# A gated MLP on one core: a reordered start, w1 sums by block, 16-bit turns and a cast moved out of the first stage

## The chip, the cores and the metric

One core of one Trainium2 chip. The metric is the time of one execution in microseconds (us), as the device reports it. An execution counts as slow when it is over 1.5% above the fastest of the same kernel. Before the change the median is 311.07 us (310.92 to 311.54, three executions).

## The reference

```python
batch, seq, dim, hidden = 16, 256, 512, 2048      # x 4096 x 512, w1 512 x 4096, w2 2048 x 512, all fp32
h = x @ w1
gate, value = np.split(h, 2, axis=-1)
h = np.maximum(gate, 0) * value
return (h @ w2).astype(np.float32)
```

## The kernel before: the parts that matter here

The kernel uses a seven-product scheme (P1 to P7) in place of eight block products for both matrix products, in fp16, over four stages of 1024 rows each. It needs sums of blocks of x (S1 to S4, on VectorE or GpSimd), of w1 (T1 to T4, on GpSimd), of w2 (also T1 to T4) and of the intermediate g. Stage 0 is special: x comes straight from its fp32 rows and is turned (transposed in blocks of 128x128) on TensorE; its first two column blocks ("plain") use ordinary products, while the sums are still missing. For stages 1 to 3, GpSimd starts a casting transfer of x to fp16 in DRAM, and transposing loads bring it in.

```python
# the order of the loads before ("fetch(i)" loads the i-th piece of w1, "fetch_first(h)" four blocks of x)
fetch(0, nc.scalar)          # w1 block 0, from ScalarE's queue
fetch_first(0)               # x blocks 0 to 3, SyncE's queue
fetch(1, nc.sync)
make_identity(nc, ident)
fetch_first(1)               # x blocks 4 to 7
fetch(2, nc.sync)            # w1 blocks 2 and 3
fetch(3, nc.sync)

def turn_first(o, h, b, ps):                       # one x block: four fp32 transposes into one PSUM bank
    for e in range(4):
        nc.tensor.transpose(ps[:, e * P:(e + 1) * P], xn[h][b][:, e * P:(e + 1) * P], ident)
    for k, copy in ((0, nc.vector.tensor_copy), (1, nc.scalar.copy)):
        copy(out=o[f"A{h + 1}{k + 1}"][:, :, b * P:(b + 1) * P], in_=ps[...])

# w1 sums of two blocks at once, on GpSimd
nc.gpsimd.tensor_tensor(op["T1"], b12, b11, op=SUB)
nc.gpsimd.tensor_tensor(op["T2"], b22, (op["T1"]), op=SUB)
nc.gpsimd.tensor_tensor(op["T3"], b22, b12, op=SUB)
nc.gpsimd.tensor_tensor(op["T4"], b21, (op["T2"]), op=SUB)
# ... cut ...
CASTS = {(0, 11): 1, (0, 13): 0, (0, 14): 2, (1, 8): 3}      # (stage, block): x of which stage is cast
FIRST_ORDER = ("P1 0, P1 1, P2 0, P2 1, P1 2, P5 0, P2 2, P6 0, ...")   # second product of stage 0
```

A matmul pair of 512 columns takes 0.43 us, eight of 256 columns 0.87 us. The second product's P5 of pair 0 needs S1 of g, which VectorE computes. And in these traces every instruction of an engine waits for those before it on the same engine, so a check or a copy that is not urgent can hold one that is (at 149 us below, ScalarE's copy starts when its check of 1.05 us is over).

## Time and profile before

| What | Value | View |
|---|---|---|
| median time | 311.07 us | executions |
| PE busy | 301.5 of 309.2 us | the page, part 1 |
| PE in the chain that ended last | 93% | the page, part 4 |
| P4 of block 2 begins | 23.30 us | timeline |
| end of the last matmul | 304.56 us | chain in order of time |

These are the page's head, its busy times and the chain by engine. PE is TensorE, PEld its weight loads, DVE is VectorE, ACT ScalarE, POOL GpSimd, SP SyncE; "issue" is time in which an engine waited for nothing that the profile shows, and a q marks an engine's sequencer.

```profile
span 309.2 us, 5211 instructions
PE 301.5 (98%) x1870; PEld 183.2 (59%) x1870; DVE 236.4 (76%) x378; ACT 177.0 (57%) x350; POOL 153.7 (50%) x186
PE 93%; DVE 2%; DMA 2%; issue 1%; SPq 0%; ACT 0%; DVEq 0%
```

TensorE bounds the kernel. What is left lies in the start. The chain in order of time (start, length, what) shows the last thing that is not TensorE:

```profile
21.96 0.69 DVE g L261
22.65 0.61 DVE cc L266
23.30 0.59 PE Y L233 x2
```

From 23.30 us on this chain is TensorE alone. I call this matmul "P4 of block 2" and use it as the milestone: the end of the kernel is P4's start, plus a fixed amount of matmul work, plus the stalls after it.

Now the timeline: start, length, engine, line, operation, output from inputs, count, and in brackets the engine's idle time before it and what ended it.

```profile
6.24 0.66 PE L448 MATMUL X<-ident,x_A 128*128 128x128 f32 x4 [0.78 <-DMA x_A<-in_x_dram]
15.57 1.36 POOL L215 TENSOR_TENSOR w_T<-w_stage 128x512 f16<-128x512 f32 x1 [5.44 <-DMA w_stage<-in_w_dram]
17.39 0.59 PE L233 MATMUL X<-x_A,w_B 128*128 128x512 f16 x2
18.64 0.59 PE L233 MATMUL X<-x_A,w_B 128*128 128x512 f16 x2 [0.23 <-ACT Y L240]
23.30 0.59 PE L233 MATMUL Y<-x_A,w_T 128*128 128x512 f16 x2 [0.47 <-DVE cc L266]
...
60.18 4.06 POOL L581 TENSOR_TENSOR v_T<-v_B,v_T 128x2048 f16<-128x2048 f16 x1
64.02 0.78 DVE L164 TENSOR_TENSOR w_stage<-g 128x1024 f16<-128x1024 f16 x1
65.22 1.04 PE L333 MATMUL W<-v_T,w_stage 128*128 128x256 f16 x8
...
149.02 1.05 ACT L179 ACTIVATE sq<-w_T 128x1024 f16<-128x1024 f16 x1
150.06 0.37 ACT L360 ACTIVATE pu<-Y 128x256 f32<-128x256 f32 x1
150.48 1.03 PE L333 MATMUL Y<-v_T,w_stage 128*128 128x256 f16 x8
```

The second x block arrives at 6.2 us, and the first block with sums starts at 17.39. At 64 us VectorE's S1 of the second product (L164) begins when GpSimd's long w2 sum is nearly over, and takes 0.78 us. At 149 us ScalarE does a 1.05 us check of a weight tile (`sq`) in front of the copy (L360) that TensorE needs; the next matmul begins 0.2 us late. The same happens in the next stage at 223 us.

### The profile page before, as it was taken

What the parts mean: (1) busy time and instruction counts of PE and PEld (TensorE: products, weight loads), DVE (VectorE), ACT (ScalarE), POOL (GpSimd) and SP (SyncE); (2) the same over time, 40 slices, a digit from 0 to 9 for tenths busy, and PEclk for the clock granted to TensorE, in tenths of its full rate; (3) what the DMA queues carried; (4) which work ended last, traced back from release to release, by engine and by line L of the source; (5) the groups of instructions that cost most, each with busy time, mean ns of one, the idle gap of its engine ahead of it and who ended that gap; (6) DMA issues with size and microseconds to landing.
All of it is one profiled execution on the core that took longest, in us unless ns stands there. A gap on an engine that the chain in (4) does not pass through costs nothing.

```text
span 309.2 us, 5211 instructions
## 1 busy us (share of the span) xinstructions
PE 301.5 (98%) x1870; PEld 183.2 (59%) x1870; DVE 236.4 (76%) x378; ACT 177.0 (57%) x350; POOL 153.7 (50%) x186
## 2 busy tenths in 40 slices
PE   7999999999999999999999999999999999999994
PEld 3844444588854444478864444458884444448883
DVE  1598888889678888887538888888536888888841
ACT  2588886445865555537855555546956555553231
POOL 2199999930048899500028889700006988700000
PEclk9999999999999999999999999999999999999999
DMA  7977696998594233001354400000325110000132
GB/s 236 355 230 251 176 232 87 196 214 149 164 303 101 69 70 68 2 0 47 127 184 105 119 0 4 0 0 15 122 103 171 37 34 1 0 3 0 70 136 72
DMA packets 37340, 32.87 MB, mean 106 GB/s; under 512 B 14400, under 2 KB 32320, under 8 KB 37184
## 3 DMA queue, kind: packets, MB, share of 16 engines
q1 hardware_dynamic: 31904, 25.70, 27.2%
q0 software_dynamic: 4352, 6.29, 11.8%
q10 hardware_dynamic: 1056, 0.52, 0.6%
q8 instruction: 15, 0.25, 0.3%
q14 instruction: 13, 0.11, 0.1%
HBM read 27.26 MB, written 12.58 MB: 129 GB/s over the span
## 4 chain that ended last, share of the span: by engine, by line
PE 93%; DVE 2%; DMA 2%; issue 1%; SPq 0%; ACT 0%; DVEq 0%
PE Y L233 26%; PE X L233 17%; PE W L233 17%; PE Y L333 14%; PE X L333 9%; PE W L333 9%; DMA x_A<-in_x_dram 2%; DVE x_S L164 1%; PE X L448 1%; DVE g L308 1%; PE X L301 1%; PE W L301 1%; PE W L448 0%; PE Y L150 0%; DVE x_S L450 0%
## 5 line engine op out<-in xcount | busy, mean ns | idle before, releaser
L233 PEld LDWEIGHTS <-w_T 128*128 128x128 f16 x496 | 48.5, 98 | 57.5 <-issue 1.0
L170 POOL TENSOR_TENSOR fold<-xh 128x1024 f32<-128x1024 f16 x16 | 30.3, 1894 | 93.1 <-DMA xh<-x 92.1
L233 PE MATMUL X<-x_A,w_B 128*128 128x512 f16 x248 | 73.7, 379 | 0.2 <-ACT Y L240 0.2
L233 PE MATMUL Y<-x_S,w_T 128*128 128x512 f16 x248 | 73.8, 379 | 0.0
L233 PEld LDWEIGHTS <-w_B 128*128 128x128 f16 x372 | 36.4, 98 | 42.6 <-issue 0.8
L240 ACT COPY Y<-X 128x512 f32<-128x512 f32 x62 | 35.4, 570 | 39.8 <-PE X L233 39.5
L260 DVE SCALAR_TENSOR_TENSOR cc<-W,pu 128x512 f32<-128x512 f32 x62 | 42.8, 691 | 19.5 <-ACT pu L254 19.5
L254 ACT ACTIVATE pu<-Y 128x512 f32<-128x512 f32 x62 | 37.0, 597 | 34.1 <-PE Y L233 32.8
L173 POOL TENSOR_TENSOR fold<-fold 128x512 f32<-128x512 f32 (+2 forms) x96 | 51.8, 540 | 7.5
L333 PEld LDWEIGHTS <-w_stage 128*128 128x128 f16 x512 | 50.0, 98 | 6.3 <-issue 0.4
L266 DVE SCALAR_TENSOR_TENSOR cc<-Y,pu 128x512 f32<-128x512 f32 x62 | 42.8, 691 | 7.2 <-PE Y L233 0.7
L261 DVE SCALAR_TENSOR_TENSOR g<-X,cc 128x512 f16<-128x512 f32 x62 | 42.9, 691 | 2.3
L276 DVE SCALAR_TENSOR_TENSOR g<-Y,cc 128x512 f16<-128x512 f32 x62 | 42.2, 681 | 1.8 <-PE Y L233 1.8
L333 PEld LDWEIGHTS <-g 128*128 128x128 f16 x384 | 37.6, 98 | 8.2
L233 PE MATMUL Y<-x_A,w_T 128*128 128x512 f16 x124 | 36.9, 379 | 0.5 <-DVE cc L266 0.5
L247 ACT ACTIVATE pu<-W 128x512 f32<-128x512 f32 x62 | 37.2, 600 | 0.2 <-ACT Y L240 0.2
L233 PE MATMUL W<-x_S,w_T 128*128 128x512 f16 x124 | 36.9, 379 | 0.0
L233 PE MATMUL W<-x_S,w_B 128*128 128x512 f16 x124 | 36.9, 379 | 0.0
L333 PE MATMUL Y<-v_T,w_stage 128*128 128x256 f16 x256 | 33.2, 272 | 0.1
L333 PE MATMUL X<-v_B,g 128*128 128x256 f16 x256 | 31.9, 273 | 0.0
L164 DVE TENSOR_TENSOR w_stage<-g 128x1024 f16<-128x1024 f16 x32 | 21.5, 686 | 0.2
L365 DVE SCALAR_TENSOR_TENSOR o<-W,pu 128x256 f32<-128x256 f32 x16 | 6.7, 422 | 18.7 <-PE W L333 18.7
(84 smaller groups left out, 283.8 us busy)
## 6 DMA issues: line engine op xcount, KB each, us to landing
out_dram<-o SPq DMA_DIRECT2D x30, 256.0 KB, 2.0
w_stage<-in_w_dram SPq DMA_DIRECT2D x14, 512.0 KB, 5.7
x<-in_x_dram POOLq DMA_DIRECT2D x4, 1024.0 KB, 12.9
xh<-x SPq DMA_DIRECT2D x16, 256.0 KB, 3.1
v_B<-in_w_dram POOLq DMA_DIRECT2D x3, 512.0 KB, 6.3
x_S<-in_x_dram SPq DMA_DIRECT2D x4, 256.0 KB, 5.5
x_A<-in_x_dram SPq DMA_DIRECT2D x3, 256.0 KB, 4.9
w_stage<-in_w_dram ACTq DMA_DIRECT2D x2, 256.0 KB, 4.6
```

The costliest lines, as they stand in the source:

```text
L164: yield eng.tensor_tensor(o[n], o[i0], o[i1], op=op)
L170: nc.gpsimd.tensor_tensor(fold, t, t, op=MULT)
L173: nc.gpsimd.tensor_tensor(fold[:, :, :m], fold[:, :, :m], fold[:, :, m:2 * m], op=ADD)
L233: nc.tensor.matmul(ps, wop[wn][:, b, self.jb * P:(self.jb + 1) * P], self.xo[xn][:, b, :], start=fresh and b == 0, stop=b == 1, skip_group ...
L240: nc.scalar.copy(out=self.Y, in_=self.X)
L247: nc.scalar.activation(self.p5, self.W, COPY, scale=GS)
L254: nc.scalar.activation(self.u2, self.Y, COPY, scale=GS)
L260: nc.vector.scalar_tensor_tensor(out=self.c12, in0=self.W, scalar=GS, in1=self.u2, op0=MULT, op1=ADD)
L261: nc.vector.scalar_tensor_tensor(out=self.g[:, self.jb, :TH], in0=self.X, scalar=0.0, in1=self.c12, op0=MAX, op1=MULT)
L266: nc.vector.scalar_tensor_tensor(out=self.c22, in0=self.Y, scalar=GS, in1=self.p5, op0=MULT, op1=ADD)
L276: nc.vector.scalar_tensor_tensor(out=self.g[:, self.jb, TH:], in0=self.Y, scalar=0.0, in1=self.c22, op0=MAX, op1=MULT)
L333: nc.tensor.matmul(ps, self.op[an][:, i], vop[wn][:, i], start=name in ("P1", "P5") and i == 0, stop=i == NJ // 2 - 1, skip_group_check=True)
```

## The change

The intent is to use TensorE's holes in the first 23 us. In words: load w1 block 0 behind two x blocks, on the same queue; put parts of the plain products between turns; cast the second half of x to fp16 before turning it; take the w1 sums of blocks 2 and 3, the first that need them, one block at a time; fill waits with warm matmuls; and cast x of stage 0 (needed only for the check of its range) in stage 2. Smaller edits go along: a check moves from pair 1 to pair 2, two w2 jobs move, and more output transfers of the last stage are split. The core, cut, with comments added for the reader:

```diff
-    fetch(0, nc.scalar)
-    fetch_first(0)
+    fetch_first(0, (0, 1))
+    ws[0] = load_w1(nc.sync, *wl[0])
+    fetch_first(0, (2, 3))
     fetch(1, nc.sync)
...
+    turn_first(xo, 0, 0, [t[:, :2 * P] for t in YS], (dve, act))     # two banks for one turn
+    turn_first(xo, 0, 1, left, (dve, act))
+    rest()
+    arm(YS[0])                                                        # warm matmuls
+    arm(YS[1])
+    plain[0].open()
+    keep_busy(2)
+    plain[0].part("gate", *first_half, half)
+    keep_busy(6)
+    turn_first(xo, 0, 2, right, (dve, act))
...
+    for b in range(3):
+        cast_first(b, pool)                                           # later x as fp16
...
-    prepare(2)
-    copy_some(3)
+    prepare(2, False)                                                 # sums of w1 block 2, then 3
+    sum_w1(6)
...
+    prepare(3, False)
+    w_sums[:4] = [w_sums[i] for i in (2, 0, 3, 1)]
+    sum_w1()
...
-            if self.t < (2 if self.s else 3):
+            if self.t in ((0, 2) if self.s else (0, 1, 2)):           # where a check stands
...
-    CASTS = {(0, 11): 1, (0, 13): 0, (0, 14): 2, (1, 8): 3}
+    CASTS = {(0, 11): 1, (0, 14): 2, (1, 8): 3, (2, 3): 0}
...
-            for n2, i0, i1, at in (("T3", "B22", "T3", (46, 50)), ("T4", "B21", "T2", (57, 58))):
+            for n2, i0, i1, at in (("T3", "B22", "T3", (46, 50)), ("T4", "B21", "T2", (57, 64))):
```

More of the change, by code (lines that the diff above doesn't have):

```diff
@@ L142, in fast_way @@
     ident = wpool.tile([P, P], F32, name="ident")
+    Y = psy.tile([P, TH], F32, name="Y", tag="Y")
     for i in range(NWARM):
-        Y = psy.tile([P, TH], F32, name="Y", tag="Y")
         nc.tensor.matmul(Y, warm_b[:, :P], warm_b[:, :TH], start=True, stop=True)
@@ L159, in x_tiles, with sum_of @@
         return o
+    SUMS_X = {"S1": ("A21", "A22", ADD), "S2": ("S1", "A11", SUB), "S4": ("A12", "S2", SUB), "S3": ("A11", "A21", SUB)}
+    def sum_of(o, n, eng=nc.vector):
+        i0, i1, op = SUMS_X[n]
+        eng.tensor_tensor(o[n], o[i0], o[i1], op=op)
     def sums_of(o, eng=nc.vector):
-        for n, i0, i1, op in (("S1", "A21", "A22", ADD), ("S2", "S1", "A11", SUB), ("S4", "A12", "S2", SUB),
-                              ("S3", "A11", "A21", SUB)):
-            yield eng.tensor_tensor(o[n], o[i0], o[i1], op=op)
+        for n in SUMS_X:
+            yield sum_of(o, n, eng)
     def look(t, at):
@@ L201, in load_rows, with load_w1, w1_ops, operands @@
         return t
-    def load_w1(eng, jb, n, u):
+    def load_w1(eng, jb, n, u, vs=(0, 1)):
         t = w_stage[:, u:u + n].rearrange("p u v -> p (u v)").rearrange("p (g e j) -> p g e j", g=2, e=4)
-        for v in range(2):
+        for v in vs:
             eng.dma_start(out=t[:, v], in_=w1_v[v, :, :, jb * P:(jb + n) * P])
         return t.rearrange("p g (k b) j -> p k b g j", k=2)
-    def w1_ops(jb, n, t):
-        js = slice(jb * P, (jb + n) * P)
-        b11, b21, b12, b22 = t[:, 0, :, 0], t[:, 1, :, 0], t[:, 0, :, 1], t[:, 1, :, 1]
-        op = {n: w[:, :, js] for n, w in wop.items()}
-        nc.gpsimd.tensor_tensor(op["T1"], b12, b11, op=SUB)
-        nc.gpsimd.tensor_tensor(op["T2"], b22, (op["T1"]), op=SUB)
-        nc.gpsimd.tensor_tensor(op["T3"], b22, b12, op=SUB)
-        nc.gpsimd.tensor_tensor(op["T4"], b21, (op["T2"]), op=SUB)
+    def w1_ops(jb, n, t, m):
+        def operands(j0, m):
+            js = slice((jb + j0) * P, (jb + j0 + m) * P)
+            b11, b21, b12, b22 = (t[:, k, :, v, j0 * P:(j0 + m) * P] for v in range(2) for k in range(2))
+            return {n: w[:, :, js] for n, w in wop.items()}, b11, b21, b12, b22
+        steps = [(0, i, n) for i in range(4)]
+        if m < n:
+            steps = [(j0, i, m) for j0, i in ((0, 0), (0, 1), (m, 0), (0, 2), (m, 1), (0, 3), (m, 2), (m, 3))]
+        def step(j0, i, m):
+            op, b11, b21, b12, b22 = operands(j0, m)
+            nc.gpsimd.tensor_tensor(op[f"T{i + 1}"], (b12, b22, b22, b21)[i], (b11, op["T1"], b12, op["T2"])[i], op=SUB)
+        w_sums.extend(lambda a=a: step(*a) for a in steps)
+        op, b11, b21, b12, b22 = operands(0, n)
         return [lambda o=o, i=i: nc.scalar.copy(out=o, in_=i)
@@ L290, in __init__, with open, part @@
             self.g, self.jb = g, jb
-        def products(self, h, a1, a2, cols=(0, TH)):
+        def open(self, X=None, W=None):
+            self.X = psx.tile([P, TH], F32, name="X", tag="X") if X is None else X
+            self.W = psw.tile([P, TH], F32, name="W", tag="W") if W is None else W
+        def part(self, which, a1, a2, cols=(0, TH)):
             js, c = slice(self.jb * P, (self.jb + 1) * P), slice(*cols)
-            if cols[0] == 0:
-                self.X = psx.tile([P, TH], F32, name="X", tag="X")
-                self.W = psw.tile([P, TH], F32, name="W", tag="W")
-            for a, gate, value in ((a1, "B11", "T3"), (a2, "B21", "B22")):
-                for ps, wn in ((self.X, gate), (self.W, value)):
-                    for b in range(2):
-                        nc.tensor.matmul(ps[:, c], wop[wn][:, b, js], a[:, b, c], start=a is a1 and b == 0,
-                                         stop=a is a2 and b == 1)
+            ps, names = (self.X, ("B11", "B21")) if which == "gate" else (self.W, ("T3", "B22"))
+            for a, wn in zip((a1, a2), names):
+                for b in range(2):
+                    nc.tensor.matmul(ps[:, c], wop[wn][:, b, js], a[:, b, c], start=a is a1 and b == 0,
+                                     stop=a is a2 and b == 1)
         def value(self):
@@ L316, in __init__ @@
             self.s, self.t = s, t
-            self.end = s == NS - 1 and t == NB // 2 - 1
+            self.end = s == NS - 1 and t != NB // 2 - 2
             o = {f"A{h + 1}{u + 1}": g[:, u * NJ // 2:(u + 1) * NJ // 2, h * TH + t * P:h * TH + (t + 1) * P]
@@ L412, in fetch, with sum_w1, prepare @@
             ws[i] = load_w1(eng, jb, n, u)
-    def prepare(i):
+    w_sums = []
+    def sum_w1(n=None):
+        for job in w_sums[:n]:
+            job()
+        del w_sums[:n]
+    def prepare(i, at_once=True):
         jb, n, _ = wl[i]
-        copies.extend((i, c) for c in w1_ops(jb, n, ws.pop(i)))
+        copies.extend((i, c) for c in w1_ops(jb, n, ws.pop(i), 1 if i == 2 else n))
+        if at_once:
+            sum_w1()
     def copy_some(n):
@@ L440, in fast_way, with fetch_first, cast_first, turn_first @@
     xn = [[t.rearrange("p a b -> p (a b)").bitcast(F32) for t in place[4 * h:4 * h + 4]] for h in range(2)]
-    def fetch_first(h):
-        for b in range(4):
-            nc.sync.dma_start(out=xn[h][b], in_=x_nat[0, h, b])
-    def turn_first(o, h, b, ps):
-        for e in range(4):
-            nc.tensor.transpose(ps[:, e * P:(e + 1) * P], xn[h][b][:, e * P:(e + 1) * P], ident)
-        for k, copy in ((0, nc.vector.tensor_copy), (1, nc.scalar.copy)):
-            copy(out=o[f"A{h + 1}{k + 1}"][:, :, b * P:(b + 1) * P],
-                 in_=ps[:, k * 256:k * 256 + 256].rearrange("p (b t) -> p b t", b=2))
+    x16_first = [halfs.tile([P, 8, P], F16, name="xh", tag="xh").rearrange("p (b q) c -> p b (q c)", b=2) for _ in range(2)]
+    ident16 = wpool.tile([P, P], F16, name="ident16")
+    half, other = (0, TH // 2), (TH // 2, TH)
+    def fetch_first(h, bs):
+        for b in bs:
+            nc.sync.dma_start(out=xn[h][b], in_=x_nat[0, h, b])
+    def cast_first(b, copy):
+        copy(out=x16_first[b // 2][:, b % 2], in_=xn[1][b])
+    def turn_first(o, h, b, places, copies):
+        rows, one = (x16_first[b // 2][:, b % 2], ident16) if h else (xn[0][b], ident)
+        for k in range(2):
+            for e in range(2):
+                nc.tensor.transpose(places[k][:, e * P:(e + 1) * P],
+                                    rows[:, (2 * k + e) * P:(2 * k + e + 1) * P], one)
+        for k in range(2):
+            copies[k](out=o[f"A{h + 1}{k + 1}"][:, :, b * P:(b + 1) * P],
+                      in_=places[k].rearrange("p (b t) -> p b t", b=2))
     def new_x():
         return psx.tile([P, TH], F32, name="X", tag="X")
-    def new_w():
-        return psw.tile([P, TH], F32, name="W", tag="W")
-    fetch(0, nc.scalar)
-    fetch_first(0)
+    def new_y():
+        return psy.tile([P, TH], F32, name="Y", tag="Y")
+    def arm(ps):
+        nc.tensor.matmul(ps, warm_b[:, :P], warm_b[:, :TH], start=True, stop=True)
+    dve, act, pool = nc.vector.tensor_copy, nc.scalar.copy, nc.gpsimd.tensor_copy
+    fetch_first(0, (0, 1))
+    ws[0] = load_w1(nc.sync, *wl[0])
+    fetch_first(0, (2, 3))
     fetch(1, nc.sync)
     make_identity(nc, ident)
-    fetch_first(1)
+    fetch_first(1, range(4))
     fetch(2, nc.sync)
     fetch(3, nc.sync)
+    dve(out=ident16, in_=ident)
     xo = x_tiles()
@@ L468, in fast_way @@
     first_half, second_half = (xo["A11"], xo["A12"]), (xo["A21"], xo["A22"])
-    half, other = (0, TH // 2), (TH // 2, TH)
+    YS, XS = [new_y(), new_y()], [new_x(), new_x()]
+    left, right = ([t[:, c:c + 2 * P] for t in XS] for c in (0, 2 * P))
+    turns = [[t.bitcast(F16)[:, c:c + 2 * P] for c in (0, 2 * P)] for t in YS]
     rest = plain_w(0)
-    turn_first(xo, 0, 0, new_w())
-    keep_busy(2)
-    turn_first(xo, 0, 1, new_x())
-    rest()
-    keep_busy(4)
-    turn_first(xo, 0, 2, new_x())
@@ L477, in fast_way @@
-    keep_busy(2)
-    turn_first(xo, 0, 3, new_w())
-    keep_busy(2)
-    plain[0].products(0, *first_half, half)
-    plain_w(1)()
+    turn_first(xo, 0, 0, [t[:, :2 * P] for t in YS], (dve, act))
[4 more added lines that the diff above has]
+    plain[0].open()
+    keep_busy(2)
+    plain[0].part("gate", *first_half, half)
+    keep_busy(6)
+    turn_first(xo, 0, 2, right, (dve, act))
+    turn_first(xo, 0, 3, left, (dve, act))
+    plain[0].part("value", *first_half, half)
@@ L482, in fast_way @@
+    rest = plain_w(1)
+    plain[0].part("gate", *first_half, other)
+    plain[0].part("value", *first_half, other)
+    rest()
     fetch(4, nc.sync)
-    plain[0].products(0, *first_half, other)
     plain[0].value()
+    plain[1].open()
+    plain[1].part("gate", *first_half)
     plain[0].gate(0)
-    plain[1].products(0, *first_half, half)
-    ps = [new_x(), new_w()]
-    for b in range(4):
-        turn_first(xo, 1, b, ps[b % 2])
-        if b == 1:
-            plain[1].products(0, *first_half, other)
-            plain[1].value()
@@ L493, in fast_way @@
-    plain[1].gate(0)
-    sums = sums_of(xo)
-    prepare(2)
-    copy_some(3)
-    fetch(5, nc.sync)
-    next(sums)
-    plain[0].products(1, *second_half, half)
-    next(sums)
-    next(sums)
-    plain[0].products(1, *second_half, other)
-    plain[0].value()
-    plain[0].gate(1)
-    prepare(3)
-    plain[1].products(1, *second_half)
+    for b in range(3):
+        cast_first(b, pool)
+    plain[1].part("value", *first_half, half)
+    turn_first(xo, 1, 0, turns[1], (act, act))
+    turn_first(xo, 1, 1, turns[0], (dve, dve))
@@ new lines, in fast_way @@
+    plain[1].part("value", *first_half, other)
+    cast_first(3, dve)
+    xo["S3"] = halfs.tile([P, 8, P], F16, name="xh", tag="xh").rearrange("p (a b) c -> p a (b c)", a=2)
+    sums = [sums_of({n: t[:, :, slice(*c)] for n, t in xo.items()}) for c in (half, other)]
+    next(sums[0])
+    turn_first(xo, 1, 2, turns[1], (act, act))
+    spare = plain[0].X.bitcast(F16)[:, :2 * P]
+    plain[0].open()
+    plain[0].part("gate", *second_half, half)
+    turn_first(xo, 1, 3, (turns[0][0], spare), (dve, act))
@@ new lines, in fast_way @@
+    plain[1].value()
+    plain[0].part("value", *second_half, half)
+    next(sums[0])
+    next(sums[1])
+    next(sums[1])
+    plain[0].part("gate", *second_half, other)
+    plain[0].part("value", *second_half, other)
+    for n in ("S4", "S3"):
+        sum_of(xo, n)
+    plain[1].gate(0)
+    prepare(2, False)
+    sum_w1(6)
+    copy_some(1)
+    plain[0].value()
+    copy_some(2)
+    plain[1].open(*reversed(YS))
+    plain[1].part("gate", *second_half)
+    prepare(3, False)
+    w_sums[:4] = [w_sums[i] for i in (2, 0, 3, 1)]
@@ L508, in fast_way, with last_plain @@
+    sum_w1()
+    fetch(5, nc.sync)
+    def last_plain():
+        plain[1].part("value", *second_half)
+        plain[1].value()
+        plain[0].gate(1)
+        plain[1].gate(1)
     LOOKX, looks = {}, []
@@ L544, in fast_way @@
     for n, at in enumerate(ats):
-        LOOKX[at] = n // 4, n % 4
+        LOOKX[at] = (n // 4 + 1) % NS, n % 4
     rows = []
@@ L551, in fast_way @@
     TAIL = 4
-    CASTS = {(0, 11): 1, (0, 13): 0, (0, 14): 2, (1, 8): 3}
+    CASTS = {(0, 11): 1, (0, 14): 2, (1, 8): 3, (2, 3): 0}
     SUMS = (10, 11, 12, 13)
-    SUMS_FIRST = (10, 11, 13, 45), (17, 22, 26, 53), (33, 37, 41, 64), (67, 72, 76, 80)
+    SUMS_FIRST = (10, 11, 13, 45), (17, 22, 26, 53), (33, 37, 41, 66), (67, 72, 76, 80)
     SUMS_AT = (10, 11, 13, 15), (22, 26, 30, 36), (46, 53, 57, 61), (70, 78, 82, 87)
@@ L595, in fast_way @@
                 if s == 0 and (n, jb) == ("P1", NPLAIN):
-                    plain[1].value()
-                if s == 0 and (n, jb) == ("P5", NPLAIN):
-                    next(sums)
-                    plain[1].gate(1)
-                if n in ("P6", "P7"):
+                    last_plain()
+                if n == "P7" or (n, jb) == ("P5", NPLAIN + 1) or n == "P6" and (s, jb) != (0, NPLAIN):
                     copy_some(1)
```

## The prediction

> **What bounds the kernel.** TensorE, nearly everywhere. The page has PE busy 301.5 of 309.2 us and 93% of the chain that ended last; the chain, in order of time, is unbroken matmul work from 23.30 us (the fourth product P4 of block 2) to 304.56 us, with pieces of 0.43 us for two 512-column matmuls and 0.87 us for eight 256-column ones. The change leaves that arithmetic alone, so only the first 23.3 us and the tail can move, and the tail (last copy at 304.58, then one output transfer) is the same for the last pair.
>
> **The start before (timeline).** PE waits for x until 4.59, then for block 1 until 6.20; x turns and plain products wait on copies; block 2's P1 begins 17.39, its P2 waits 0.23 for ScalarE's copy, its P4 waits until 23.30 for VectorE's L266. PE had about 16 us of needed work between 4.6 and 23.3, with 1.1 us of warm matmuls: about 1.6 us of holes. VectorE is continuous from 13.76 to 23.25 and is what releases P4. Its x sums took 0.70 us alone (S1) but 1.65 and 1.53 us (S2, S4) once GpSimd's w1 sums had begun at 15.57. The Trainium skill ("GPSIMD Engine Reference", "Specifications") says the two engines share SBUF interfaces and contend for VectorE instructions with two SBUF inputs; this trace agrees.
>
> **What the change does.**
> - w1 behind two x blocks on one queue: landings follow bytes, about 0.7 to 0.78 us per 256 KB. x blocks 0 and 1 should land near 4.0 and 4.8 instead of 4.48 and 6.20; w1 block 0 at 5.6/6.35 instead of 4.85/6.39; everything later as before (w1 for blocks 2 and 3 at 13.92/15.42).
> - First turns start about 4.3, limited by the seven warm matmuls at 0.43 us; two banks per turn let ScalarE copy beside VectorE (before it waited, 4.6 us in total).
> - Later x: three casts on GpSimd, idle there (estimate 0.7 us each from its 0.37 us for half the size), one on VectorE; transposes of 0.109 us become about half (estimate).
> - x sums by halves: S1 and S2 mostly before GpSimd's sums start, saving VectorE about 1 us; S4 and S3 still contended.
> - w1 sums by block: first T1 ready near 16.2 instead of 16.93, T2 17.0 instead of 18.5.
> - Cast of x0 moved to stage 2: less DMA near 55 to 75 us; PE did not wait there.
>
> **Sum.** Walking the orders with these durations: block 2's P1 near 16.1, P2 near 17.95 (ScalarE's Y copy again), P4 ready on PE at 21.8 but VectorE (S4, S3, three gates, c12, g, c22) ends about 22.5. So 0.8 to 1.4 us saved of 23.3, all on the critical path; nothing after it.
>
> Predicted 309.9 us, 8 in 10 between 309.0 and 310.8. Faster by over 2%: 0.01; within 2%: 0.98; slower: 0.01.
>
> **Signs that it is right.** Block 2's P4 starts 0.8 to 1.4 us earlier; the stretch from there to the last matmul stays 281.3 us within 0.3; S1/S2 near 0.7 us per whole; VectorE, not DMA, releases P4.
>
> **What would make it wrong.** GpSimd's casts late or slow, holding the second x half; the fp16 transposes not faster; T1 for blocks 4/5 (slack only 1.2 us before: ready 22.97, P5 at 24.16) now late, so that PE is stopped by GpSimd and the gain is lost; VectorE less contended than thought, giving up to 1.8 us.

## The result

| | before | changed |
|---|---|---|
| median of the fast runs | 311.09 us (310.92 to 311.54, 4) | 310.15 us (309.85 to 310.37, 4) |
| ratio, 95% interval | | 0.9967 (0.995 to 0.9984) |
| span of the profiled execution | 309.2 us | 308.4 us |
| P4 of block 2 begins | 23.30 us | 22.25 us |
| P4's start to the end of the last matmul | 281.26 us | 281.66 us |

A ratio here is the mean time of one kernel's fast runs over that of the other's of the same rounds, so it is not quite the ratio of the medians. The time is within the predicted range; by the 2% measure it is "same".

The head of the changed kernel's page:

```profile
span 308.4 us, 5218 instructions
PE 301.3 (98%) x1866; PEld 182.3 (59%) x1866; DVE 235.4 (76%) x381; ACT 177.4 (58%) x351; POOL 155.1 (50%) x193
PE 95%; DMA 2%; DVE 1%; SPq 1%; issue 0%; ACT 0%; DVEq 0%
```

Its chain in order of time:

```profile
2.80 5.48 DMA x_A<-in_x_dram
8.32 0.45 PE X L481 x2
8.79 0.44 DVE x_A L484
9.28 0.66 PE X L481 x4
9.93 0.44 PE W L314 x4
```

And its timeline at the places shown of before:

```profile
8.32 0.65 PE L481 MATMUL X<-ident,x_A 128*128 128x128 f32 x4 [0.58 <-DMA x_A<-in_x_dram]
16.52 0.73 POOL L227 TENSOR_TENSOR w_T<-w_stage 128x256 f16<-128x256 f32 x1 [3.18 <-DMA w_stage<-in_w_dram]
16.59 0.59 PE L245 MATMUL X<-x_A,w_B 128*128 128x512 f16 x2
18.31 0.59 PE L245 MATMUL X<-x_A,w_B 128*128 128x512 f16 x2
21.34 0.68 DVE L278 SCALAR_TENSOR_TENSOR cc<-Y,pu 128x512 f32<-128x512 f32 x1
22.25 0.59 PE L245 MATMUL Y<-x_A,w_T 128*128 128x512 f16 x2
...
60.10 4.06 POOL L651 TENSOR_TENSOR v_T<-v_B,v_T 128x2048 f16<-128x2048 f16 x1
62.98 1.73 DVE L165 TENSOR_TENSOR w_stage<-g 128x1024 f16<-128x1024 f16 x1
64.77 1.05 PE L347 MATMUL W<-v_T,w_stage 128*128 128x256 f16 x8 [0.42 <-DVE w_stage L165]
...
149.36 0.38 ACT L374 ACTIVATE pu<-Y 128x256 f32<-128x256 f32 x1 [0.49 <-PE Y L347]
149.65 1.05 ACT L184 ACTIVATE sq<-w_T 128x1024 f16<-128x1024 f16 x1
```

The start gained 1.05 us by the milestone: from the turn of x block 3 at 9.28 us on, TensorE waits no longer than 0.13 us at a time until P4. Then three things happen behind P4. The two stalls of 0.198 us by a check are gone (the copy at 149.36 now comes before the check). A new stall of 0.59 us stands at 64 us: TensorE and VectorE arrive a microsecond earlier, GpSimd does not: its w2 sum ends at 64.16 us (64.24 before). VectorE's S1 now starts 1.18 us before that end instead of 0.22 us, and takes 1.73 instead of 0.78 us; both times it ends 0.55 us after GpSimd's sum. A smaller one, 0.19 us in two parts, stands at 76 us. The sum, 1.05 + 0.40 - 0.59 - 0.19 = 0.67 us, is what the end of the last matmul moved (304.56 to 303.91, 0.65 us). The span became shorter by 0.8 us; the other 0.15 us lie behind the last matmul, in the last output transfers. That part lasts from 4.32 to 4.79 us over all the profiles, so two kernels with the same last matmul can differ by some tenths of a microsecond. These stalls are measured as the gap between the starts of two neighbouring matmuls less their normal distance.

One reading differs at once from the prediction: the loads. "Everything later as before" is false in this execution. Landings in us, worked out from the trace (issue order of the changed kernel):

```
                      x0    x1    w1 block 0    x2    x3    w1 blocks 2,3 (second part)
before (two queues)   4.48  6.20  4.85  6.39    7.06  7.92  15.42
changed (one queue)   3.65  4.28  5.84  6.89    8.28  8.96  16.38
```

### The profile page after: what moved, and what is told of

Its sections match the earlier page's. It is cut to its first block, busy times and chain, and to the rows that moved or that the text cites. A ratio compares the mean times of both kernels' runs of the same rounds, so it can differ in the third digit from the quotient of the medians.

```text
span 308.4 us, 5218 instructions
## 1 busy us (share of the span) xinstructions
PE 301.3 (98%) x1866; PEld 182.3 (59%) x1866; DVE 235.4 (76%) x381; ACT 177.4 (58%) x351; POOL 155.1 (50%) x193
## 4 chain that ended last, share of the span: by engine, by line
PE 95%; DMA 2%; DVE 1%; SPq 1%; issue 0%; ACT 0%; DVEq 0%
PE Y L245 26%; PE X L245 17%; PE W L245 17%; PE Y L347 14%; PE W L347 9%; PE X L347 8%; DMA x_A<-in_x_dram 2%; PE W L314 1%; PE X L314 1%; DVE w_stage L165 1%; PE Y L314 1%; PE X L481 0%; PE Y L481 0%; SPq L212 0%; SPq L471 0%; DVE g L288 0%
## 5 line engine op out<-in xcount | busy, mean ns | idle before, releaser
L245 PE MATMUL Y<-x_S,w_T 128*128 128x512 f16 x220 | 65.4, 379 | 0.0
L252 ACT COPY Y<-X 128x512 f32<-128x512 f32 x62 | 35.4, 571 | 38.1 <-PE X L245 37.9
L165 DVE TENSOR_TENSOR w_stage<-g 128x1024 f16<-128x1024 f16 x32 | 22.4, 716 | 0.2
```

The source lines that it names most:

```text
L165: eng.tensor_tensor(o[n], o[i0], o[i1], op=op)
L245: nc.tensor.matmul(ps, wop[wn][:, b, self.jb * P:(self.jb + 1) * P], self.xo[xn][:, b, :], start=fresh and b == 0, stop=b == 1, skip_group ...
L252: nc.scalar.copy(out=self.Y, in_=self.X)
```

## The experiments

All twelve gave correct results. The yardsticks over all of them: the landing of x block 2 (x2; five pieces of 256 KB have been asked for by then in either order), P4's start, the start of the last matmul, and the stalls behind P4. The last column is the distance from P4's start to the last matmul's start less 280.57 us; that number is the distance before (280.97) less its two check stalls of 0.20 us. One profile stands behind each row, and the times of one kernel's executions spread wider than most of these differences. "after_again" is the changed kernel, unaltered, on the chip of the second group. Kernels of one group ran on one chip with the same runs of before; between groups only the ratios can be compared.

```
group kernel        ratio   95% interval      x2     P4     last matmul  stalls behind P4
  -   before                                  7.06   23.30  304.27       0.40
  -   changed       0.9967  0.9950 to 0.9984  8.28   22.25  303.63       0.81
  1   w0_act        0.9993  0.9953 to 1.0033  7.12   22.49  303.26       0.20
  1   w0_act_late   0.9945  0.9931 to 0.9958  6.96   22.48  303.25       0.20
  1   no_warm       0.9986  0.9955 to 1.0016  7.06   21.14  302.76       1.05
  1   turns_f32     0.9978  0.9965 to 0.9992  7.96   23.20  304.56       0.79
  2   after_again   0.9971  0.9958 to 0.9985  7.80   21.95  303.29       0.77
  2   sums_pair     0.9967  0.9953 to 0.9981  8.88   23.56  304.34       0.21
  2   cast2_late    0.9979  0.9965 to 0.9992  8.02   22.06  304.01       1.37
  2   before_looks  0.9994  0.9980 to 1.0007  7.05   23.18  304.09       0.34
  3   cast_rush     0.9993  0.9975 to 1.0011  7.20   22.11  303.92       1.24
  3   fixes         0.9946  0.9933 to 0.9960  7.68   21.98  303.37       0.82
  3   best          0.9942  0.9926 to 0.9958  7.02   21.46  302.85       0.82
  3   best_cast     0.9981  0.9968 to 0.9995  7.10   21.34  304.26       2.36
```

The theory after the result: (a) the change makes TensorE's chain shorter at the start by filling its holes; (b) what it brings is partly given back, because the chains of GpSimd and of the transfers did not get shorter. The rival to (a) was that one part alone (the early x) carries the gain; the rival to (b) that the new stalls have causes of their own.

For the stall at 64 us the kept traces leave little room for a rival. In the fourteen profiles 32 of VectorE's sums of 128x1024 fp16 tiles start while a sum of GpSimd is running. They take from 0.69 to 1.90 us, and 31 of them end 0.545 to 0.553 us after that GpSimd sum (one 0.59 us after), whenever they started; alone such a sum takes 0.68 us. So VectorE's sum is not slowed in proportion: these traces look as if it waits until GpSimd's is over. S1 at 64 us, and with it TensorE, then depends on when GpSimd's w2 sum ends, and starting S1 earlier gains nothing.

### w0_act: w1 block 0 from ScalarE's queue again

```diff
-    ws[0] = load_w1(nc.sync, *wl[0])
+    ws[0] = load_w1(nc.scalar, *wl[0])
```

> The changed kernel with the two transfers of w1 block 0 issued from ScalarE's queue again, as before the change. Theory (one queue for x and the narrow w1 pieces moves fewer bytes early than two): x block 1 lands late again (about 6.2 instead of 4.28 us), but x block 2 lands near 7.1 instead of 8.28 and all later pieces about 1 us earlier (w1 for blocks 2 and 3 near 15.4 instead of 16.38). PE then has the turn of block 1 and 1.3 us of warm matmuls still to do before the turn of block 2, so only 0.2 to 0.5 us are gained: P4 of block 2 near 21.8 to 22.1 instead of 22.25, time 0 to 0.5 us lower. Rival (the late landings were an accident of that execution, or come of the order of the pieces): x block 2 lands at about 8.3 here too, P4 at 22.2 or later.

The landings came as the first theory said: x2 at 7.12, w1 for blocks 2 and 3 at 15.35. P4 at 22.49 did not: it is later than the 21.8 to 22.1 expected. With x1 at 6.27, TensorE finishes the warm matmuls only after x2 is there, so an earlier x2 buys nothing. It also bears on the rival to (a): x0, x1 and x2 land here as late as before the change (4.55, 6.27 and 7.12 us), and P4 is still 0.81 us earlier than before, so the early x alone does not carry the gain. The end came earlier all the same: the last matmul starts at 303.26 against 303.63, because the stall at 64 us is absent. GpSimd starts its w1 sums with their load, at 15.50 instead of 16.52, and is done with w2 at 63.78 instead of 64.16; S1 takes 1.13 us. The time is unclear: four runs of 309.66 to 310.24 and two of 312.54 and 313.91 with no lower clock; what made those two long stays open.

### w0_act_late: the same behind ScalarE's table load

```diff
+    nc.scalar.copy(out=ident16[:, :1], in_=warm_b[:, :1])
-    ws[0] = load_w1(nc.sync, *wl[0])
+    ws[0] = load_w1(nc.scalar, *wl[0])
```

> As w0_act, but a one-column copy on ScalarE comes first, so that its table load runs before the two transfers are issued (about 2.1 us instead of 0.73). Theory: x blocks 0 and 1 keep their early landing (about 3.7 and 4.4 us), and with two queues x block 2 still lands near 7.1 to 7.5. Then PE starts its unbroken run about 0.8 us earlier: P4 of block 2 near 21.4, time 0.4 to 0.9 us below the changed kernel's (part is lost again to the GpSimd contention near 64 us). Rival: no gain in landing, P4 at 22.2.

The landing of x2 (6.96) and the ratio (0.9945, five runs within 0.7 us) came, but not by the expected way. x1 landed at 5.39 and not at 4.4, and P4 is at 22.48 and not 21.4. The timeline of TensorE in this run shows why:

```profile
6.34 1.05 PE L495 MATMUL Y<-warm 128*128 128x512 f16 x2
7.20 0.41 PE L150 MATMUL Y<-warm 128*128 128x256 f16 x2
7.45 0.60 PE L314 MATMUL X<-x_A,w_B 128*128 128x256 f16 x4
7.88 0.82 PE L150 MATMUL Y<-warm 128*128 128x256 f16 x6
8.54 0.60 PE L481 MATMUL X<-ident,x_A 128*128 128x128 f32 x4
```

The warm matmuls start at 6.34, at half rate for the first two (0.43 us each, as at the very start of every run), and the turn of x2, which had landed at 6.96, waits for them until 8.54. Two things are mixed here. TensorE runs at half rate until about 7.2 us in this profile: the transposes of x1 start 0.213 us apart, those of x2 0.109. In the changed kernel's first profile and in w0_act the full rate comes at about 5.3 us, in the fourteen profiles between 4.6 (or a little before) and 7.2. From the turn of x1 on, the half rate costs about 0.87 us (an estimate: four transposes 0.104 us longer each, two matmuls of 512 columns 0.21 us each, and 0.03 us); the rest is the warm work itself. What sets that moment was not tested. What was gained lies behind P4: stalls of 0.20 us in place of 0.81, as in w0_act. So an execution in which TensorE is later and GpSimd's w2 sum ends earlier (63.76 against 64.16) ends no later: its last matmul starts at 303.25, against 303.63 and 303.29 in the two profiles of the changed kernel. That is a strong sign for (b). The ratio, 0.0022 to 0.0026 (some 0.7 to 0.8 us) below the changed kernel's, is more than these starts explain, and the intervals overlap.

### no_warm: the ten warm matmuls between the turns taken out

```diff
-    arm(YS[0])
-    arm(YS[1])
-    keep_busy(2)
-    keep_busy(6)
```

> The changed kernel without the ten warm matmuls between the first turns (two of 512 and eight of 256 columns; the seven at the very start stay). Theory: they only fill time in which PE waits for x block 2 (8.28 us), so without them the time is the same within 0.2 us and matmul pieces keep 0.43 us for two of 512 columns. Rival: the idle time between 5.6 and 8.3 us lowers the PE clock, the matmuls after 8.3 us take up to twice as long for some microseconds, and the time rises by 1 us or more.

This run came with a surprise: with the same order on one queue x2 landed at 7.06. So the late landing of the changed kernel is not fixed; it varies between executions. Without the fill TensorE could use it, and P4 is at 21.14, 1.1 us earlier than in the changed kernel. The clock did not drop: the pairs after 8.07 us keep their 0.43 us. The Trainium skill ("TensorE: Matmul & The Clock Gate", "HAM oscillation — how this bites in real kernels") gives as the rule no TensorE gaps over about 3.4 us; the largest gap in this run's first 30 us after the start is 0.46 us, and nothing slowed; no run here has a gap of that length, so the figure itself was not tested. Nor did the fill bring the full rate earlier: it came at about 6.5 us here, and between 4.9 and 7.1 us in the other one-queue profiles, which have it. The warm matmuls in the waits are thus worth nothing here, and cost time when x2 is early. But of the 1.1 us only 0.87 arrive at the last matmul, because the stalls behind P4 are 0.24 us longer. At 64 us 0.37 us remain, and there is a new stall:

```profile
28.22 0.62 ACT L231 CAST w_B<-w_stage 128x512 f16<-128x512 f32 x1 [0.66 <-DMA w_stage<-in_w_dram]
29.38 0.59 PE L245 MATMUL X<-x_A,w_B 128*128 128x512 f16 x2 [0.29 <-ACT Y L252]
```

ScalarE's copy of w1 block 8 waits for its load and stands in front of the copy of PSUM that TensorE needs: 0.46 us. The load is late because its place in the staging buffer is freed by GpSimd's last sum of blocks 2 and 3 (the waits of the issuing queue name GpSimd's `w_T`; in sums_pair, without the new order of sums, the transfer is issued at 22.40 us). Before, that transfer was issued at 21.77 us (landing 26.07); in the changed order, with T1 and T2 of blocks 4 and 5 put in between, at 23.78 here (landing 28.20) and 24.67 in the changed kernel's first profile. The times of this run are unclear: two of its six (313.15 and 311.71) are far above the others.

### turns_f32: the second half of x turned as fp32

```diff
-        rows, one = (x16_first[b // 2][:, b % 2], ident16) if h else (xn[0][b], ident)
+        rows, one = xn[h][b], ident
...
-    for b in range(3):
-        cast_first(b, pool)
-    cast_first(3, dve)
```

> The changed kernel with the second half of x turned as fp32 straight from the loaded rows: no casts, 16 transposes of 128x128 fp32. Theory (PE is unbroken after 9.28 us, so PE time counts): transposes go from about 0.055 to 0.109 us, 0.87 us more on PE, less about 0.2 us of waits for the casts: P4 of block 2 0.5 to 0.8 us later than 22.25, time 0.3 to 0.8 us higher. Rival (the casts cost as much as they save): time within 0.15 us of the changed kernel.

From the turn of x3 to P4 the changed kernel takes 12.97 us in both of its profiles; here it takes 13.67 (9.53 to 23.20). So the 16-bit turns are worth 0.70 us on TensorE, as expected: eight transposes go from 0.72 us in the first line to 1.04 us in the second, start to start from 0.055 to 0.109 us.

```profile
12.40 0.72 PE L481 MATMUL Y<-ident,xh 128*128 128x128 f16 x8
```

```profile
12.62 1.04 PE L481 MATMUL Y<-ident,x_S 128*128 128x128 f32 x8
```

The ratio, 0.9978, lies about 0.001 above the changed kernel's two, with intervals that overlap; x3 landed at 9.39 in this execution, so its P4 also holds 0.25 us of late start.

### Changed again (after_again): the yardstick

> The changed kernel, unaltered, executed again on the chip of the other three runs, as their yardstick and as a second look at the landings. Theory now (the three one-queue profiles so far landed x block 2 at 7.06, 7.96 and 8.28 us with the same order of transfers): the landing varies from execution to execution, and PE starts its unbroken run with it; so this profile has x block 2 anywhere between 7.0 and 8.5 us, P4 of block 2 from 21.4 to 22.3, and the ratio to before stays 0.995 to 0.998. Rival (one queue is always about 1 us late): x block 2 at 8.0 or later again.

x2 landed at 7.80, P4 at 21.95, ratio 0.9971: the first theory holds. Over all profiles, x2 landed between 6.96 and 7.12 us in the six with w1 block 0 on a second queue, and between 7.06 and 8.88 (mean 7.86) in the eight with one queue. The Trainium skill ("DMA: Bandwidth & Descriptors", "Issuing engines are not separate DMA queues") says that issuing from several engines at once saves only sequencer time; the saving is seen here (x2 is asked for at 1.80 us with the second queue and at 2.80 with one), but it alone does not explain the landings, since with one queue all of the first six pieces were asked for by 3.35 us. In three of the two-queue profiles (w0_act_late, best, best_cast) x2 overtook the second piece of w1 block 0; but all six pieces together are no less steady: they had landed by 7.80 to 7.97 us with two queues, and by 7.89 to 9.60 with one. Why is open: in three of the one-queue profiles single packets took over 1.2 us between 4 and 9.5 us, and none over 0.61 us in the two-queue ones, but the latest landing of all (8.88) had no packet over 0.63 us. The stalls behind P4 differ between the two profiles of the same kernel (0.59 at 64 us in one, 0.31 at 29.5 and 0.24 at 64 in the other), and so does P4, but their sums nearly agree: 0.81 and 0.77.

### sums_pair: w1 sums of blocks 2 and 3 as one pair again

```diff
-        copies.extend((i, c) for c in w1_ops(jb, n, ws.pop(i), 1 if i == 2 else n))
+        copies.extend((i, c) for c in w1_ops(jb, n, ws.pop(i), n))
-    prepare(2, False)
-    sum_w1(6)
+    prepare(2)
-    prepare(3, False)
-    w_sums[:4] = [w_sums[i] for i in (2, 0, 3, 1)]
-    sum_w1()
+    prepare(3)
```

> The changed kernel with GpSimd's w1 sums for blocks 2 and 3 taken as one pair again (T1, T2, T3, T4 of 512 columns each). Theory: T1 is ready about 0.6 us later and T2 about 1.1 us later than by block; PE reaches P6 of block 2 about 0.3 to 0.9 us before T2 is there and stalls that long, so P4 of block 2 is 0.4 to 1.0 us later than in after_again for the same landing of the loads. By the end part is regained, since the stall of 0.59 us near 64 us shrinks when PE comes later: time 0 to 0.6 us above after_again. Rival (sums by block are worth nothing, PE is held by its own work): P4 within 0.2 us.

The stall is there, at P6 of block 2, waiting for T2 from GpSimd:

```profile
18.54 1.49 POOL L227 TENSOR_TENSOR w_T<-w_stage,w_T 128x512 f16<-128x512 f32 x1
20.09 0.61 PE L245 MATMUL Y<-x_S,w_T 128*128 128x512 f16 x2 [0.49 <-POOL w_T L227]
```

The distance from the turn of x3 to P4 grows from 12.97 to 13.59 us, 0.62 us. And all of it comes back: the stalls at 29.5 and 64 us are gone, 0.21 us remain behind P4 in place of 0.77, and the time is that of the changed kernel in the same rounds (310.33 against 310.25 us). In this profile x2 was the latest of all, 8.88 us, and P4 1.6 us later than in the changed kernel again; the last matmul starts only 1.05 us later. So the sums by block do what they are meant to do at P6, and bring nothing that can be seen at the end of these runs.

### cast2_late: the cast of x for stage 2 one block later

```diff
-    CASTS = {(0, 11): 1, (0, 14): 2, (1, 8): 3, (2, 3): 0}
+    CASTS = {(0, 11): 1, (0, 15): 2, (1, 8): 3, (2, 3): 0}
```

> The changed kernel with the cast of x of stage 2 issued from GpSimd one block later, behind the two 4.1 us sums of w2 instead of before them. Theory (the stall near 64 us comes of VectorE's first sum of the second product meeting GpSimd's second w2 sum): those sums end 0.5 us earlier, VectorE's sum takes about 1.1 instead of 1.73 us, the stall falls from 0.59 to 0 to 0.25 us, the time by 0.2 to 0.5 us. Rival (the stall has another cause, for instance PE's own order): the stall stays 0.4 to 0.6 us.

The stall at 64 us is gone and S1 takes 0.93 us. That is not a clean verdict: TensorE had already lost 0.58 us at 29.6 us to ScalarE's late copy, and came later. The gain expected did not come; the time is 310.82 against 310.25 us of the changed kernel in the same rounds. It was lost to a stall I had not expected, near 85 us:

```profile
83.32 1.42 DVE L165 TENSOR_TENSOR x_S<-x_S,x_A 128x1024 f16<-128x1024 f16 x2 [2.91 <-issue]
84.99 0.41 DVE L384 SCALAR_TENSOR_TENSOR o<-Y,pu 128x256 f32<-128x256 f32 x1
85.46 0.60 PE L347 MATMUL Y<-v_T,g 128*128 128x256 f16 x4 [0.43 <-DVE o L384]
```

VectorE sits idle for the transposing loads of the next stage (the one it needs lands at 83.24 us; the view's "issue" does not name it), does two sums, and only then the output row on which TensorE waits: 0.59 us. In the changed kernel VectorE's sums start at 82.27 and 82.06 us in the two profiles, here at 83.32, in the kernel before at 83.03. In the kernel before, with 83.03, no stall stands here, since TensorE came later.

### before_looks: of the whole change only the check that moved

```diff
-            if self.t < (2 if self.s else 3):
+            if self.t in ((0, 2) if self.s else (0, 1, 2)):
```

> The kernel before with one line of the change alone: in the stages after the first, ScalarE's check of a weight tile stands after P4 of pairs 0 and 2 instead of 0 and 1. Theory: the two PE stalls of 0.198 us at 150.2 and 223.2 us, where ScalarE's 1.05 us check stood in front of the copy that PE waited for, are gone; nothing else moves; 0.3 to 0.5 us less than before. Rival (those stalls vanish for another reason, such as the cast of x0 moved): both stalls stay, time within 0.15 us of before.

Both stalls, at 150 and 223 us, are gone, so the mechanism is shown:

```profile
149.82 0.38 ACT L360 ACTIVATE pu<-Y 128x256 f32<-128x256 f32 x1 [0.49 <-PE Y L333]
150.10 1.05 ACT L179 ACTIVATE sq<-w_T 128x1024 f16<-128x1024 f16 x1
150.50 1.04 PE L333 MATMUL Y<-v_T,w_stage 128*128 128x256 f16 x8
```

The size was missed: the ratio is 0.9994 and its interval includes 1. In this profile the transposing loads came at 83.40, 0.37 us later than in the profile of before, and a stall of 0.34 us at 85 us took back most of it.

### cast_rush: the cast of x0 back in stage 0

```diff
-    CASTS = {(0, 11): 1, (0, 14): 2, (1, 8): 3, (2, 3): 0}
+    CASTS = {(0, 11): 1, (0, 13): 0, (0, 14): 2, (1, 8): 3}
```

> The changed kernel with the cast of x0 back in the first stage, as before the change. Theory (PE now runs about 1 us ahead of the chains that GpSimd and the transfers set, so what keeps these busy in the first stage costs time): GpSimd's two w2 sums end 0.5 us later, and the transposing loads of the next stage, which VectorE waits for, end 0.5 to 1 us later than with the cast gone. So the stall near 64 us is at least as long as in the changed kernel (0.2 to 0.7 us), and a new one of 0.2 to 0.7 us stands near 85 us; ratio to before 0.9975 to 1.0 against 0.9971 of the changed kernel run again. Rival (the cast is idle work, no part of the gain): no stall near 85 us, ratio 0.996 to 0.9975.

The theory holds in both places. S1 takes 1.90 us and the stall at 64 us is 0.76 us; VectorE's sums near 83 us start about a microsecond later than in the changed kernel, and a stall of 0.27 us stands at 85 us:

```profile
62.84 1.90 DVE L165 TENSOR_TENSOR w_stage<-g 128x1024 f16<-128x1024 f16 x1
64.80 1.05 PE L347 MATMUL W<-v_T,w_stage 128*128 128x256 f16 x8 [0.60 <-DVE w_stage L165]
83.24 1.42 DVE L165 TENSOR_TENSOR x_S<-x_S,x_A 128x1024 f16<-128x1024 f16 x2 [2.59 <-issue]
```

The ratio is 0.9993 (six runs, of which two are near 312 us, so its interval is wide: 0.9975 to 1.0011), against 0.9967 and 0.9971 of the changed kernel; the intervals overlap, so how much of the gain hangs on this one line is not settled. In its profile the last matmul starts at 303.92, 0.3 to 0.6 us later than in the changed kernel's two and 0.35 us earlier than before.

### fixes: two repairs of what gives the gain back

```diff
-    FIRST_ORDER = ("... P1 2, P5 0, P2 2, P6 0, ...
+    FIRST_ORDER = ("... P1 2, P2 2, P5 0, P6 0, ...
-                if n == "P7" or ... or n == "P6" and (s, jb) != (0, NPLAIN):
+                if n == "P7" or ... or n == "P6" and (s, jb) not in ((0, NPLAIN), (0, 5)):
```

> The changed kernel with two repairs of what gives the gain back later, and its start as it is: (1) ScalarE's first copy of w1 for block 8, which waited for its load in front of a copy that PE needed (stall of 0.306 us at 29.5 us in the second profile of the changed kernel, 0.579 and 0.457 in two others), is put one place later; (2) in the first stage's second product P2 of pair 2 goes before P5 of pair 0, so that VectorE's contended sum has 0.87 us more. Theory: the stalls near 29 and 64 us are gone; about 0.3 to 0.6 us less than the changed kernel, ratio 0.9950 to 0.9965. Rival (the time comes back further on, as with the later cast): a stall near 85 us of 0.2 us or more takes it, ratio as the changed kernel's, 0.9965 to 0.9975.

The first repair worked: the load of w1 block 8 landed as late as in the changed kernel again (28.84 and 28.86 us), but no copy of w1 now stands before ScalarE's urgent copy (L252, at 29.10), and there is no stall near 29 us. (Its absence alone would show nothing: the changed kernel's first profile has none there either.) The second failed as built: P2 of pair 2 now follows its P1 at once and waits for ScalarE's copy of the same bank, 0.61 us, so one stall took the place of another. The ratio is 0.9946, lower than expected from a profile whose last matmul starts at 303.37, no earlier than in the changed kernel again (303.29). The profiled execution is one of the two slowest of its five (310.16 us); in this profile 4.73 us lie behind the last matmul, against 4.32 in changed again. What made the others faster was not profiled and stays open.

### best: the repairs, w1 block 0 as in w0_act_late, no fill

> The two repairs with w1 block 0 on ScalarE's queue behind its table load and no warm matmuls between the turns. Theory: x block 2 lands at about 7.0 us in every execution and PE is free then, so its unbroken run starts about 1 us earlier than in the changed kernel; P4 of block 2 near 21.2. If nothing later holds it: ratio to before 0.991 to 0.994. Rival (PE then meets the transposing loads of the next stage, which end near 82.3 to 83.4 us whatever PE does): a stall of 0.5 us or more near 84 us, ratio 0.9935 to 0.996.

Its edit is that of w0_act_late, no_warm and fixes together. P4 is at 21.46 and the last matmul at 302.85, 0.78 us earlier than in the changed kernel's first profile. My exchange of P5 and P2 costs its stall of 0.61 us here too; what the old order would have cost in its place was not run (no_warm, with the old order and P4 at 21.14, lost 0.37 us there):

```profile
63.59 0.36 ACT L360 COPY Y<-X 128x256 f32<-128x256 f32 x1 [0.43 <-PE X L347]
64.00 0.82 PE L347 MATMUL X<-v_B,g 128*128 128x256 f16 x6 [0.45 <-ACT Y L360]
```

No stall stands at 84 us; the rival was wrong in that, and its ratio right. Fast runs of 309.10 to 310.21 us (a sixth, 313.75, is just over 1.5% above the fastest, so left out; runs such as 313.91 in w0_act and 313.15 in no_warm, 1.4 and 1.3% above their fastest, stayed in, which raises those kernels' ratios), ratio 0.9942. It beats the kernel before. Against the changed kernel its ratio is 0.25 to 0.29% lower, but that it is better is not shown: the two were not run in the same rounds and the intervals of their ratios overlap. The same holds of w0_act_late, which needs two lines.

### best_cast: the next stage's cast two blocks earlier

```diff
-    CASTS = {(0, 11): 1, (0, 14): 2, (1, 8): 3, (2, 3): 0}
+    CASTS = {(0, 9): 1, (0, 14): 2, (1, 8): 3, (2, 3): 0}
```

> As best, with the cast of x for the next stage issued from GpSimd two blocks earlier. Theory: its load lands about 8 us earlier than 65 us, the transposing loads that wait for it end well before 82 us, no stall near 84 us; ratio 0.990 to 0.9935 and below best. Rival (the earlier cast delays the w2 loads and with them GpSimd's sums): a stall of 0.5 us or more between 60 and 70 us, no better than best.

The rival was right about the loads and the size of the stall, but not about GpSimd's sums, which begin at 59.20 us as in best (59.27). With the earlier cast transfer in flight the last load of w2 takes longer, which landed at 61.70 instead of 59.33 us, and TensorE itself waits for it:

```profile
61.74 0.61 PE L347 MATMUL X<-v_B,g 128*128 128x256 f16 x4 [1.36 <-DMA v_B<-in_w_dram]
```

## Why the prediction was right, and where it was not

- **Bound and place, right.** The whole effect lies in the first 22 us and in stalls of TensorE; its work is the same. P4 moved by 1.05 us in one profile and 1.35 in the other, against 0.8 to 1.4 predicted. The time, 310.15 us, is inside 309.0 to 310.8, 0.25 us above the point. That it is so close is in part luck: P4 came in range by another path than the predicted one (TensorE ready later than the 21.8 us forecast, VectorE earlier than its 22.5), and behind P4 gains and losses that had not been priced nearly cancel (the next points).
- **"Everything later as before": wrong in this execution.** x2 landed at 8.28 instead of near 7.1 us and all later pieces about 1 us late. Over eight one-queue profiles the mean is 7.86. The early landing of x0 and x1 was right (3.65 and 4.28; predicted 4.0 and 4.8).
- **"VectorE, not DMA, releases P4": wrong.** TensorE itself was the limit, and its unbroken run began with the landing of x2: VectorE had finished at 22.02. I had summed VectorE's S4 as contended. Since GpSimd's sums started later than assumed (16.52 us), S4 took 0.69 us alone, and only S3 (1.25) was contended. The sharing of SBUF interfaces that the Trainium skill states ("GPSIMD Engine Reference", "Specifications") was the right mechanism; the time of its onset was wrong. S1 and S2 by halves took about 0.8 us per whole (0.42 per half), near the 0.7 forecast.
- **"The stretch from there to the last matmul stays 281.3 us within 0.3": wrong by 0.1.** It is 281.66. The term was taken as zero; it is a sum of 0.40 us gained by the moved check, which I had not priced, and 0.78 us lost at 64 and 76 us. "Nothing after it" was thus the step that failed, by two errors of opposite sign. GpSimd's chain did not move with TensorE's. The 64 us stall is shown to depend on their distance by w0_act, w0_act_late and sums_pair, in which it is gone when TensorE is later or GpSimd earlier. Of the 0.19 us at 76 us, present in the changed kernel and every variant of it, but not in before_looks, the cause was not tested by a run. The traces point at one of the small edits: in the changed kernel TensorE waits there for VectorE's sums (L165, 75.52 us), in front of which now stands a w2 job that the change moved (L690, 74.93 us, 0.6 us); before, all four of these jobs are over at 74.7. GpSimd is idle there in the changed kernel's first profile.
- **"PE did not wait there" for the cast of x0: right of the kernel before, wrong as a price.** cast_rush shows that the cast, free at the old pace, goes with a stall at 85 us and a longer one at 64 us at the new pace (one profile; how much of it reaches the time is not settled).
- **Prices, right.** GpSimd's casts took 0.66 us each (estimate 0.7), 16-bit transposes half of fp32 ones, 0.70 us in all (turns_f32).
- **The risk named for GpSimd, half right.** Not T1 for blocks 4 and 5 came late, but the place in the staging buffer that the reordered sums free later (24.67 instead of 21.77 us), through a load and a copy on ScalarE.
- **What was not tested alone:** the split outputs, the early x0 and x1 alone (w0_act only shows that most of the start's gain comes without them), and the products between turns.

## What to carry to other kernels

When one engine bounds the kernel and its start is made shorter, ask which other chains keep their own clock (here GpSimd's sums, the staging buffer they free, a casting transfer), and where the faster engine will meet them: each cost nothing before and a few tenths of a microsecond after. Price every edit of a change, the one-line move of a check too; in the profiles here it took away 0.40 us of stalls, where the whole new start brought 1.05. And look at a second profile of the same kernel before a landing time is called a fact.

## What the Trainium skill lacked or had wrong

- "DMA: Bandwidth & Descriptors" ("Issuing engines are not separate DMA queues") says that several issuing engines save only sequencer time, and has nothing on how much a landing varies. Here x2 landed at 6.96 to 7.12 us in six profiles with a second queue, and at 7.06 to 8.88 us in eight with one; the runs do not show why, so the page is not shown to be wrong.
- "TensorE: Matmul & The Clock Gate" ("Part 4: PE-mode transpose") gives durations of single transposes but no rate for a row of them. Here 128x128 transposes start 0.055 us apart in fp16 and 0.109 us in fp32, once TensorE is at its full rate.
